# z's last four weight blocks and six of the output projection's in float32 products, without kept halves; the experts' early tiles five instead of three

## Chip, cores and metric

One Trainium2 chip, one core of it. The metric is the device time of one execution in microseconds (us); the kernel before has three runs, of which the median counts, and one profiled execution.

## What is computed

Two transformer blocks in float32 on 256 tokens of 1,024 features. The first block (stick-breaking attention, an RWKV-7 time mix and a gated feed-forward) is not touched. The second block, cut to what matters:

```python
u, z, xbc, dt = split(modulate(x) @ w_in)          # second input projection
y_pool = pool_mixer(u)                             # 256 columns
y_ssd  = rms(ssd(conv(xbc), dt) * silu(z)) * norm_w   # 768 columns, rms in 4 groups of 192
x = x + gate * (concat(y_pool, y_ssd) @ w_out)     # output projection
h = modulate(x)
x = x + gate * hier_moe(h, w13, w2)                # router, then 32 experts, top 2 in one group
```

## The kernel before

The work runs in stages on 128 tokens by up to 512 columns. Most large products are made in a reduced float format: a value is split into its rounding hi and the remainder lo (`wsplit`, L334, and `split_to`, L298: ScalarE rounds, L300, VectorE subtracts, L301), and `mm3` (L329) adds the three products hi*hi, hi*lo and lo*hi at L330 to L332. The experts' products (L1508 ph, L1571 pyo) take plain float32.

After the first block come four stages. *The second input projection* (`project`, L1130): for each chunk of 128 columns the weights, loaded two chunks to a tile (L350), are split and multiplied into `pi` (24 matmuls of 256 columns); `projected` (L1140) then makes the causal convolution, first ScalarE (L1146, `cva`), then three taps on VectorE (L1149), then the silu (L1150). The dt columns go through four small transposes (`pdt`, L1191) after the last chunk. *z*: `dense_rows` (L857) loads w_z in four tiles of two k each (L876), and multiplies block by block while the SSD (L1208 to L1241) runs between its products. Its argument `stag` says that the last four k keep their split halves, so that token block 0 can finish before block 1 uses the same halves. `fin_z` takes the silu of z, multiplies y, makes the four squares, a reciprocal root by some 13 small VectorE steps (L229 to L234), the scaling L1277, and turns y by transposes (`pyt`, L1281) into hi and lo (L1286, L1287). *The output projection*: the same `dense_rows` on w_out, with all eight k split, four of them kept in ring R; `fin_out` adds the result to x (L1374, L1375) and makes the router's product (`plg`, L1388). *The experts*: a tile of weights is 1 MB, six tiles an expert.

Expert tiles are loaded ahead of need by `fetch` (L1084), which SyncE issues in program order together with all other weights. `ORDER` names, one letter a tile, the buffers of the first 17: E is a ring of its own that exists early (`RING3` tiles), b pairs of half-size blocks, r the four-tile ring of all weight loads, R a ring of `RING2` tiles that exists from the output projection on; three more use a, w and x. `SOON` says how many tiles are fetched at three places (after the first chunks of the input projection, after the last, after the SSD), `EARLY` how many ahead of the output projection. A tile beyond these waits until its buffer is given back. The tile framework puts instructions of an engine in an order by its own planner, except where `issue_after` forces one.

Of the kernel before, what the change touches and what calls it, by code (L numbers as in the profile page):

```python
# [8 lines left out]
F32 = mybir.dt.float32  # L9
F32R = mybir.dt.float32r  # L10
# [21 lines left out]
BIG = 3.0e38  # L32
NEG = -3.0e38
RING = 4
RING2 = 5
RING3 = 3
ZROWS = 11
DT = 0
UP = 0
# [4 lines left out]
PO = 2  # L44
PD = 4
PZ = 2
PW = 1
WOSTAG = 4
SO = 6
SD = 5  # L50
WBUFS = 4
NB = 14
MIXG = 8
HALVES = 8
ORDER = "EEEbbbbRrrrrRRbRR"
EARLY = 8
ONCE = "awx"
SCHED = {}
RES = (29, 30)
R0 = (1,1,1,0,0,0)  # L60
SOON = (5, 5, 6)
AFT = (9, 12)
SCW = 4
WARM = (16, 4, 5, 2, 9)
PN = "mttp"
# [8 lines left out]
def two_blocks(ctx: ExitStack, tc: tile.TileContext, a: dict, out: bass.AP, dump=None, stop=""):  # L74
# [3 lines left out]
    def D_(name, ap):  # L78
        if dump is not None:
            dump(name, ap)  # L80
# [27 lines left out]
    def nm(s):  # L108
        uid[0] += 1
        return f"{s}{uid[0]}"  # L110
# [34 lines left out]
    def small(s, shape, dt=F32, tag=None, bufs=2):  # L145
        return (sc if shape[-1] <= SCW and len(shape) == 2 and shape[0] == P else ph["pool"]).tile(shape, dt, tag=tag or s, name=nm(s), bufs=bufs)
# [119 lines left out]
    def halves(t, n=512):  # L266
        return [t[:, 0:n], t[:, n : 2 * n]]
# [61 lines left out]
    def mm3(ps, lh, ll, rh, rl, first, last):  # L329
        pe.matmul(ps, lhsT=lh, rhs=rh, start=first, stop=False)  # L330
        pe.matmul(ps, lhsT=lh, rhs=rl, start=False, stop=False)  # L331
        pe.matmul(ps, lhsT=ll, rhs=rh, start=False, stop=last)  # L332

    def wsplit(src, n, alloc=None, eng=dve):  # L334
        hi, lo = (alloc or wblk)("wh"), (alloc or wblk)("wl")
# [136 lines left out]
    def hv(t, i):  # L472
        return t[:, i * 256 : (i + 1) * 256]
# [380 lines left out]
        D_(f"mTh{g}", mT[0][g]); D_(f"mTl{g}", mT[1][g])  # L854


    def dense_rows(w, nk, xT, finish, stag=2, keep=None, n=1024, pos=0, fill=None, after=()):  # L857
# [12 lines left out]

        pairs = list(range(0, nk, 2))
        first, last = pairs[: len(pairs) - stag // 2], pairs[len(pairs) - stag // 2 :]
        for n_, k0 in enumerate(first[:pos] + last + first[pos:]):
            t = raw("wrows")
            v = t[:, : 2 * n].rearrange("p (k c) -> p k c", k=2)
            sync.dma_start(out=t[:, : 2 * n], in_=w[k0 // 2])  # L876
            for j in range(2):
                with ExitStack() as st:
                    for at, ins in after:
                        if 2 * n_ + j >= at:  # L880
                            st.enter_context(tc.issue_after(ins))
                    hi, lo = wsplit(v[:, j, :], n, keep if k0 in last else wblk)
                if k0 in last:
                    kept.append((k0 + j, hi, lo))
                else:
                    go(0, k0 + j, hi, lo)
                    go(1, k0 + j, hi, lo)
        for k, hi, lo in kept:
            go(0, k, hi, lo)
        finish(0, acc[0])  # L890
        for k, hi, lo in kept:
            go(1, k, hi, lo)
        if fill:
            fill()
        finish(1, acc[1])
# [179 lines left out]
    def raw2(s_, dt=F32):  # L1075
        return ph["pool"].tile([P, 2048], dt, tag="raw2", name=nm(s_), bufs=RING2)
# [169 lines left out]
    fetch_n(SOON[2])  # L1246


    yT = act_T("mixT")
    for c in range(2):  # L1250
        ps = psm("ppool")
        for j in range(2):
            hs = slice(64 * j, 64 * j + 64)
            pe.matmul(ps[hs, 0:256], lhsT=wpool[hs, c, :], rhs=pw[hs, c, 16:272], start=True, stop=True)
        t = small("yp", [P, 256], bufs=2)
        dve.tensor_scalar(t, ps[:, 0:256], prm("pool_scale_2", c), None, op0=ALU.mult)
        split_to(atv(yT[0], c), atv(yT[1], c), t)
        D_(f"yp{c}", t)


    z_done = []

    def fin_z(tb, acc):
        sz = blk("sz")
        with tc.issue_after(last_exp.ins) if ZA else ExitStack():
            for hf in range(2):
                act.activation(sz[:, hf * 512 : hf * 512 + 512 - 256 * hf], acc[hf], AF.Silu)
        y = ysd[tb][:, 0:768]
        dve.tensor_tensor(y, y, sz[:, 0:768], ALU.mult)
        ss = small("gss", [P, 4])  # L1270
        for g in range(4):
            act.activation(sink[:, 0:192], y[:, g * 192 : g * 192 + 192], AF.Square, accum_out=ss[:, g : g + 1])
        v = small("gsv", [P, 4])
# [3 lines left out]
        z_done.append(dve.tensor_tensor(y3, y3, rk.rearrange("p (g o) -> p g o", o=1).to_broadcast([P, 4, 192]), ALU.mult).ins)  # L1277
        for g, n in ((0, 4), (1, 2)):
            pt = psm("pyt")
            for j in range(n):  # L1280
                pe.transpose(pt[:, j * P : (j + 1) * P], y[:, (4 * g + j) * P : (4 * g + j + 1) * P], ident)  # L1281
            for j in range(n):
                i = 4 * g + j
                src = pt[:, j * P : (j + 1) * P]
                hi, lo = (atv(yT[x], 2 + i, tb * P, tb * P + P) for x in range(2))
                act.activation(hi, src, AF.Copy, scale=prm("ssd_norm_w_2", i))  # L1286
                dve.scalar_tensor_tensor(lo, src, prm("ssd_norm_w_2", i), hi.bitcast(F32), op0=ALU.mult, op1=ALU.subtract)  # L1287
# [8 lines left out]
    kept = []  # L1296

    def keep(s_):
        if not kept:
            kept.extend(halves(raw2(s_, F32R), 1024))  # L1300
        return kept.pop(0)

    hn = [[blk("hnh", F32R), blk("hnl", F32R)] for _ in range(2)]
    lg = small("lg", [P, 2, 40], bufs=1)
# [456 lines left out]
```

## Time and profile before

| | us |
|---|---|
| runs | 1121.05, 1121.59, 1119.37 |
| median of the three | 1121.05 |
| the profiled execution | 1120.24 |
| its span on the core | 1118.5 |
| outside the span | 1.7 |

The mean granted TensorE clock of the profiled execution is 0.987. The span counts from the first to the last recorded instruction; times in rows are from its start. A TensorE row's length is that of one pipelined matmul, so of a series the steps between starts count, as the chain of waits gives them.

### The profile page before, as it was taken

The page shows a single profiled execution, that of the slowest core. Times are in us where ns is not written, and L with a number is a line of the kernel's source. Part 1 is how long each engine was busy: PE and PEld are TensorE (multiplying, and loading weights), DVE is VectorE, ACT ScalarE, POOL GpSimd, SP SyncE. Part 2 cuts the span into 40 slices and gives each one's busy share as a digit, 9 for nine tenths or more (in the row PEclk, how much of TensorE's full clock was granted, in tenths as well). Part 3 has the DMA queues.
Part 4 walks back from the last instruction along what each step waited for, and adds up shares of the span by engine and source line. Part 5 has one row for each costly group of instructions (what it writes and reads, how often), then busy time and mean ns, then how long its engine had stood idle before and what let it go on. Part 6 is the DMA issues. An engine that isn't in the chain of part 4 may idle for free.

```text
span 1118.5 us, 17553 instructions
## 1 busy us (share of the span) xinstructions
PE 1053.5 (94%) x7022; PEld 732.2 (65%) x7022; DVE 592.2 (53%) x1228; ACT 403.6 (36%) x713; POOL 82.0 (7%) x155
## 2 busy tenths in 40 slices
PE   8999999998799999999999889999999999999895
PEld 7988778896599999877997653444444444433332
DVE  5575975768778874555985653323232323222213
ACT  5454443454444444435665341121111111111113
POOL 4001600003200000004100000000000000000000
PEclk9999989999999999999999999999999999999998
DMA  9654520256566773636664599999999999999993
GB/s 328 219 214 163 193 81 16 101 181 234 196 256 227 263 287 121 253 113 227 247 208 151 184 326 419 410 419 416 416 421 416 415 420 417 416 419 417 417 418 150
DMA packets 57717, 313.01 MB, mean 280 GB/s; under 512 B 8864, under 2 KB 11040, under 8 KB 28064
## 3 DMA queue, kind: packets, MB, share of 16 engines
q1 hardware_dynamic: 53712, 286.50, 65.6%
q0 software_dynamic: 3456, 25.17, 6.1%
q8 instruction: 57, 0.93, 0.3%
q10 hardware_dynamic: 464, 0.17, 0.1%
q14 instruction: 28, 0.23, 0.1%
HBM read 310.77 MB, written 1.05 MB: 279 GB/s over the span
## 4 chain that ended last, share of the span: by engine, by line
PE 73%; DMA 15%; DVE 7%; ACT 2%; issue 2%; POOL 1%; SPq 0%; DVEq 0%; POOLq 0%; ACTq 0%
PE ph L1508 15%; DMA wexp<-in_w_dram 11%; PE pyo L1571 7%; PE acc L331 3%; PE acc L332 3%; PE acc L330 3%; PE moe L1589 2%; PE pga L1353 2%; DVE wl L301 2%; PE pfg L330 2%; PE pfg L331 2%; PE pfg L332 2%; PE pfu L331 2%; PE pfu L330 2%; PE pfu L332 2%
## 5 line engine op out<-in xcount | busy, mean ns | idle before, releaser
L1508 PE MATMUL ph<-wexp,xg 128*64 128x512 f32 x1024 | 229.5, 595 | 9.6 <-DMA wexp<-in_w_dram 9.0
L1508 PEld LDWEIGHTS ph<-wexp,xg 128*64 128x64 f32 x1024 | 71.8, 137 | 159.8 <-issue 129.3
L1571 PE MATMUL pyo<-wexp,gy 128*64 128x512 f32 x512 | 116.9, 599 | 2.6 <-DVE gy L1565 2.1
L1515 DVE TENSOR_TENSOR gy<-gy,ph 128x256 f32<-128x256 f32 x32 | 13.5, 421 | 152.2 <-ACT gy L1514 152.2
L1576 DVE SCALAR_TENSOR_TENSOR gy<-pyo,gs,g2h 128x512 f32<-128x512 f32 x32 | 24.0, 751 | 103.5 <-PE pyo L1571 103.5
L1571 PEld LDWEIGHTS pyo<-wexp,gy 128*64 128x64 f32 x512 | 34.1, 137 | 62.5 <-issue 53.7
L1514 ACT ACTIVATE gy<-ph 128x256 f32<-128x256 f32 x32 | 12.3, 383 | 165.0 <-PE ph L1508 165.0
L301 DVE TENSOR_TENSOR wl<-wrows,wh 128x1024 fp32r<-128x1024 f32 (+1 forms) x42 | 51.4, 1241 | 24.9 <-ACT wh L300 24.6
L301 DVE TENSOR_TENSOR wl<-wff,wh 128x1024 fp32r<-128x1024 f32 x44 | 55.1, 1253 | 17.2 <-ACT wh L300 17.1
L1580 ACT CAST yh<-gy 64x512 fp32r<-64x512 f32 x32 | 19.8, 618 | 115.6 <-DVE gy L1576 115.6
L300 ACT CAST wh<-wff 128x1024 fp32r<-128x1024 f32 x44 | 46.0, 1045 | 36.4 <-DMA wff<-in_w_ffn_dram 21.5
L300 ACT CAST wh<-wrows 128x1024 fp32r<-128x1024 f32 (+1 forms) x46 | 45.3, 1009 | 30.5 <-PE acc L331 21.7
L330 PE MATMUL pfg<-h2Th,wh 128*128 128x256 f32 x176 | 50.7, 288 | 0.1
L332 PE MATMUL pfg<-h2Th,wl 128*128 128x256 f32 x176 | 50.0, 284 | 0.0
L331 PE MATMUL pfu<-h2Tl,wh 128*128 128x256 f32 x176 | 49.9, 284 | 0.0
L330 PE MATMUL pfu<-h2Th,wh 128*128 128x256 f32 x176 | 49.9, 284 | 0.0
L332 PE MATMUL pfu<-h2Th,wl 128*128 128x256 f32 x176 | 49.9, 283 | 0.0
L331 PE MATMUL pfg<-h2Tl,wh 128*128 128x256 f32 x176 | 49.9, 283 | 0.0
L1353 PE MATMUL pga<-sel,hnh 128*128 128x256 f32 x128 | 33.1, 305 | 8.7 <-DVE sel L1347 7.0
L332 PE MATMUL pi<-h3Th,wl 128*128 128x256 f32 (+1 forms) x136 | 38.7, 284 | 1.8 <-DVE wl L301 1.8
L331 PE MATMUL pi<-h3Tl,wh 128*128 128x256 f32 (+1 forms) x136 | 38.6, 284 | 0.0
L330 PE MATMUL pi<-h3Th,wh 128*128 128x256 f32 (+1 forms) x136 | 38.6, 284 | 0.0
(555 smaller groups left out, 2593.1 us busy)
## 6 DMA issues: line engine op xcount, KB each, us to landing
wexp<-in_w_dram SPq DMA_DIRECT2D x134, 1024.0 KB, 15.2
wexp<-in_w_dram SPq DMA_DIRECT2D x116, 512.0 KB, 12.7
wada<-in_w_ada_dram POOLq DMA_DIRECT2D x24, 1024.0 KB, 5.3
wff<-in_w_ffn_dram SPq DMA_DIRECT2D x22, 1024.0 KB, 5.9
wrows<-in_w_ffn_down_dram SPq DMA_DIRECT2D x11, 1024.0 KB, 5.4
wg<-in_w_in_dram SPq DMA_DIRECT2D x8, 1024.0 KB, 4.9
wi<-in_w_in_dram SPq DMA_DIRECT2D x8, 1024.0 KB, 5.6
wrw<-in_w_in_dram SPq DMA_DIRECT2D x6, 1024.0 KB, 9.3
```

The source lines that it names most:

```text
L300: act.copy(hi, src)
L301: eng.tensor_tensor(lo, src, hi.bitcast(F32), ALU.subtract)
L330: pe.matmul(ps, lhsT=lh, rhs=rh, start=first, stop=False)
L331: pe.matmul(ps, lhsT=lh, rhs=rl, start=False, stop=False)
L332: pe.matmul(ps, lhsT=ll, rhs=rh, start=False, stop=last)
L1353: return pe.matmul(ps, lhsT=hn[tb][part][:, k * P : (k + 1) * P], rhs=sel[tb].rearrange("p (e j s) -> p e j s", e=GE, j=2)[:, :, 0, :], st ...
L1508: last = pe.matmul(ph_[64 * t_ : 64 * t_ + 64, :], lhsT=xg[k // 4][:, (k % 4) * 256 + el * CAP : (k % 4) * 256 + el * CAP + CAP], rhs=wa[k ...
L1515: dve.tensor_tensor(g, g, ph_[:, 256:512], ALU.mult)
L1571: last = pe.matmul(py_[64 * t_ : 64 * t_ + 64, :], lhsT=gT[:, (kc % 2) * P + (kc // 2) * 64 : (kc % 2) * P + (kc // 2) * 64 + 64], rhs=wb[ ...
L1576: dve.scalar_tensor_tensor(y32, py_, gs, g2h, op0=ALU.mult, op1=ALU.mult)
L1580: act.copy(y[hi], y32[hi])
L1589: last = pe.matmul(acc[tb][hf], lhsT=sT[:, tb * P : (tb + 1) * P], rhs=ys[hf], start=(e == 0), stop=(e == E - 1))
```

## The change

The last four k of z are no longer split: the raw float32 weight rows are multiplied with `h3f`, the sum of the activations' hi and lo, in one float32 product each (L868 of the changed kernel). The output projection has code of its own, `out_rows`: y is kept in float32 (`yf`) for k 0, 1 and 4 to 7, which are multiplied with the raw rows (L1481), and in hi and lo (`y23`) for k 2 and 3, whose weights are still split. k 0 and 1 (the pool's part) come first for both token blocks; then y of block 0 is scaled and turned, k 2 and 3 of block 0, y of block 1 is scaled and turned, the rest of block 0, and block 1. The rings hold five E and three R tiles instead of three and five; `SOON` fetches seven tiles at the first place instead of five.

```diff
-RING2 = 5
-RING3 = 3
+RING2 = 3
+RING3 = 5
-PW = 1
-WOSTAG = 4
-ORDER = "EEEbbbbRrrrrRRbRR"
-EARLY = 8
+ORDER = "EEEEEbbbbRRRrrbrr"
+EARLY = 9
-SOON = (5, 5, 6)
-AFT = (9, 12)
+SOON = (7, 7, 8)
...
+                if lo is None:
+                    pe.matmul(acc[tb][hf], lhsT=hv(whole, k % 4)[:, t0:t1], rhs=hi[:, sl], start=ndone[tb] == 0, stop=ndone[tb] == nk - 1)
+                    continue
...
+                if whole is not None and k0 in last:
+                    kept.append((k0 + j, v[:, j, :], None))
+                    continue
...
-    dense_rows(a["w_z"], KC, h3T, fin_z, 4, lambda s_: ph["pool"].tile([P, 768], F32R, tag="keep", name=nm(s_), bufs=8), 768, PZ)
+    h3f = pconst("h3f", [P, 1024])
+    dve.tensor_tensor(h3f, h3T[0][1].bitcast(F32), h3T[1][1].bitcast(F32), ALU.add)
+    dense_rows(a["w_z"], KC, h3T, fin_z, 4, None, 768, PZ, whole=h3f)
...
-    dense_rows(a["w_out_2"], KC, yT, fin_out, WOSTAG, keep, pos=PW, after=list(zip(AFT, z_done)))
+    def out_rows():
...
+        w23 = [wsplit(w[k], 1024) for k in (2, 3)]
+        fetch_n(EARLY + RING2)
...
+                if k in (2, 3):
...
+                    last = mm3(acc[tb][hf], yh, yl, halves(hi)[hf], halves(lo)[hf], False, False)
+                else:
+                    last = pe.matmul(acc[tb][hf], lhsT=hv(yf[k // 4], k % 4)[:, t0:t1], rhs=halves(w[k])[hf], start=k == 0, stop=k == KC - 1)
...
+        for k in range(2):
+            for tb in range(2):
+                go(tb, k)
+        scaled(0)
+        turn = turned(0)
+        for k in (2, 3):
+            last = go(0, k)
+        with tc.issue_after(turn.ins):
+            scaled(1)
+        with tc.issue_after(last.ins):
+            turned(1)
+        for k in range(4, KC):
+            go(0, k)
+        fin_out(0, acc[0])
+        for k in range(2, KC):
+            go(1, k)
+        fin_out(1, acc[1])
```

How it moves instructions, in three places. The first is SyncE's queue in the second input projection, before (wi are the projection's tiles, wexp the experts'; a half tile has 1024 columns):

```order
L1092 DMA wexp_5838<-in_w_2_dram 128x2048
L1092 DMA wexp_5840<-in_w_2_dram 128x2048
L1092 DMA wexp_5842<-in_w_2_dram 128x2048
L350 DMA wi_6010<-in_w_in_dram 128x2048
L350 DMA wi_6082<-in_w_in_dram 128x2048
L1098 DMA wexp_5844<-in_w_2_dram 128x1024
L1098 DMA wexp_5845<-in_w_2_dram 128x1024
L1098 DMA wexp_5848<-in_w_2_dram 128x1024
L1098 DMA wexp_5849<-in_w_2_dram 128x1024
L350 DMA wi_6154<-in_w_in_dram 128x2048
L350 DMA wi_6226<-in_w_in_dram 128x2048
```

and in the changed kernel:

```order
L1097 DMA wexp_5838<-in_w_2_dram 128x2048
L1097 DMA wexp_5840<-in_w_2_dram 128x2048
L1097 DMA wexp_5842<-in_w_2_dram 128x2048
L1097 DMA wexp_5844<-in_w_2_dram 128x2048
L1097 DMA wexp_5846<-in_w_2_dram 128x2048
L1103 DMA wexp_5848<-in_w_2_dram 128x1024
L1103 DMA wexp_5849<-in_w_2_dram 128x1024
L1103 DMA wexp_5852<-in_w_2_dram 128x1024
L1103 DMA wexp_5853<-in_w_2_dram 128x1024
L347 DMA wi_6014<-in_w_in_dram 128x2048
L347 DMA wi_6086<-in_w_in_dram 128x2048
```

The two late input tiles (wi_6010 and wi_6082 before, wi_6014 and wi_6086 now) had three expert tiles ahead of them and now have five and two pairs of halves.

The second is ScalarE in the same stage, around the first split of the late input tile, before (CAST wh is a split, the ACTIVATE from pi the convolution's start, into BT or CT the silu):

```order
L1150 ACTIVATE BT_5649<-cva_5897 128x256
L300 CAST wh_6013<-wi_6010 128x1024
L1146 ACTIVATE cva_5969<-pi_5940,par 128x256
L1150 ACTIVATE BT_5649<-cva_5932 128x256
L300 CAST wh_6048<-wi_6010 128x1024
L1146 ACTIVATE cva_6004<-pi_5975,par 128x256
L1150 ACTIVATE CT_5650<-cva_5969 128x256
```

and in the changed kernel:

```order
L1155 ACTIVATE BT_5649<-cva_5901 128x256
L1151 ACTIVATE cva_5973<-pi_5944,par 128x256
L1155 ACTIVATE BT_5649<-cva_5936 128x256
L1155 ACTIVATE CT_5650<-cva_5973 128x256
L1151 ACTIVATE cva_6008<-pi_5979,par 128x256
L297 CAST wh_6017<-wi_6014 128x1024
L1155 ACTIVATE CT_5650<-cva_6008 128x256
```

The split of the late tile (wh_6013 before, wh_6017 now) stood ahead of the convolution of the chunk two before its own (pi_5940); now it stands behind that of the chunk right before its own (pi_5979). On VectorE the remainder wl of this split stands behind that convolution's three taps in the same way.

The third is TensorE in the output projection, where y's transposes come, before (acc are the sums of the two token blocks by two halves):

```order
L330 MATMUL acc_6771<-wh_6790,mixTh_6490 128x512
L331 MATMUL acc_6771<-wl_6791,mixTh_6490 128x512
L332 MATMUL acc_6771<-wh_6790,mixTl_6492 128x512
L1281 MATMUL pyt_6650<-ident,ysd_6308 128x128 x4
L1281 MATMUL pyt_6663<-ident,ysd_6308 128x128 x2
L330 MATMUL acc_6768<-wh_6824,mixTh_6490 128x512
L331 MATMUL acc_6768<-wl_6825,mixTh_6490 128x512
```

and in the changed kernel:

```order
L1481 MATMUL acc_6645<-wrows_6647,mixT_6494 128x512
L1481 MATMUL acc_6646<-wrows_6647,mixT_6494 128x512
L1293 MATMUL pyt_6694<-ident,ysd_6312 128x128 x4
L1293 MATMUL pyt_6705<-ident,ysd_6312 128x128 x2
L327 MATMUL acc_6643<-wh_6655,mixT_6496 128x512
L328 MATMUL acc_6643<-wl_6656,mixT_6496 128x512
L329 MATMUL acc_6643<-wh_6655,mixT_6496 128x512
```

Before, the products ahead of the transposes are hi/lo ones of k 0 and 1; now they are float32 ones (L1481), eight in all, and the hi/lo products of k 2 follow.

## Rows read from the trace of the kernel before

**Rows 1.** The page: busy time, traffic by slice (40), the last chain by engine.

```profile
PE 1053.5 (94%) x7022; PEld 732.2 (65%) x7022; DVE 592.2 (53%) x1228; ACT 403.6 (36%) x713; POOL 82.0 (7%) x155
...
GB/s 328 219 214 163 193 81 16 101 181 234 196 256 227 263 287 121 253 113 227 247 208 151 184 326 419 410 419 416 416 421 416 415 420 417 416 419 417 417 418 150
...
PE 73%; DMA 15%; DVE 7%; ACT 2%; issue 2%; POOL 1%; SPq 0%; DVEq 0%; POOLq 0%; ACTq 0%
```

**Rows 2.** The chain of waits, 940 to 1000 us: start, us, what.

```profile
943.11 6.87 PE ph L1508 x32
...
952.62 17.41 DMA wexp<-in_w_dram
...
970.10 13.19 DMA wexp<-in_w_dram
```

**Rows 3.** By window: length; PE, PEld, DVE, ACT, POOL busy; granted clock, DMA share, GB/s.

```profile
680.00:720.00 40.00, 39.48 (x203) 17.51 (x199) 12.36 (x22) 7.84 (x15) 0.00 (x0) 1.00 1.01 415
```

**Rows 4.** Timeline of SyncE's queue, 606 to 665 us: first start, time over all, issues.

```profile
646.85 9.46 SPq L1098 DMA_DIRECT2D wexp<-in_w_dram  x6
659.37 2.04 SPq L1092 DMA_DIRECT2D wexp<-in_w_dram  x2
```

**Rows 5.** The chain of waits, first expert matmuls.

```profile
657.39 7.09 PE ph L1508 x32
```

**Rows 6.** By window: second input projection, z, output projection.

```profile
538.00:569.42 31.42, 31.42 (x262) 31.36 (x262) 28.90 (x47) 21.75 (x37) 0.00 (x0) 1.00 0.55 191
569.49:608.58 39.09, 39.09 (x234) 31.91 (x233) 25.06 (x48) 21.39 (x45) 0.00 (x0) 1.00 0.54 187
608.58:642.12 33.54, 29.25 (x134) 22.47 (x132) 21.75 (x61) 15.86 (x42) 0.19 (x1) 0.95 0.49 177
```

**Rows 7.** Timeline of ScalarE, 543.5 to 550.8 us.

```profile
543.56 1.05 ACT L300 CAST wh<-wi 128x1024 fp32r<-128x1024 f32 x1 [0.95 <-PE pi L331]
...
546.44 1.05 ACT L300 CAST wh<-wi 128x1024 fp32r<-128x1024 f32 x1 [1.06 <-PE pi L331]
547.40 0.56 ACT L1146 ACTIVATE cva<-pi,par 128x256 f32<-128x256 f32 x1
```

**Rows 8.** Timeline of VectorE, 543.5 to 551.7 us (x3: three taps together).

```profile
544.64 1.23 DVE L301 TENSOR_TENSOR wl<-wi,wh 128x1024 fp32r<-128x1024 f32 x1
545.78 1.51 DVE L1149 SCALAR_TENSOR_TENSOR cva<-pi,par,cva 128x255 f32<-128x255 f32 x3
```

**Rows 9.** Timeline of SyncE's queue, 518 to 545 us.

```profile
518.89 1.46 SPq L1092 DMA_DIRECT2D wexp<-in_w_dram  x3
523.83 6.17 SPq L350 DMA_DIRECT2D wi<-in_w_in_dram  x2
```

**Rows 10.** By window, the first expert's loads.

```profile
658.00:668.00 10.00, 8.90 (x46) 3.19 (x44) 1.99 (x11) 2.88 (x6) 0.00 (x0) 1.00 0.82 291
```

**Rows 11.** The chain of waits in the output projection.

```profile
622.53 0.43 PE acc L331
...
625.85 0.23 PE acc L330
...
627.02 0.66 PE pyt L1281 x6
...
634.66 0.54 PE ptr L1380 x4
...
636.56 0.82 PE plg L1388 x8
```

**Rows 12.** TensorE's waits, 600 to 645 us: in all, times, longest.

```profile
PE pyt L1281 <- DVE gsv L1274: 2.2, 1, 2.2
PE acc L331 <- DVE wl L301: 1.5, 1, 1.5
```

**Rows 13.** By window, around an idle stretch of TensorE.

```profile
256.90:260.20 3.30, 0.02 (x2) 0.01 (x1) 3.30 (x4) 0.78 (x1) 3.30 (x3) 1.00 0.87 330
261.00:264.00 3.00, 3.00 (x12) 2.20 (x11) 3.00 (x4) 1.97 (x3) 3.00 (x3) 0.54 0.95 371
```

More of the change, by code (lines that the diff above doesn't have):

```diff
@@ L331, in mm3 @@
         pe.matmul(ps, lhsT=lh, rhs=rl, start=False, stop=False)
-        pe.matmul(ps, lhsT=ll, rhs=rh, start=False, stop=last)
+        return pe.matmul(ps, lhsT=ll, rhs=rh, start=False, stop=last)
     def wsplit(src, n, alloc=None, eng=dve):
@@ L854, in two_blocks, with dense_rows @@
         D_(f"mTh{g}", mT[0][g]); D_(f"mTl{g}", mT[1][g])
-    def dense_rows(w, nk, xT, finish, stag=2, keep=None, n=1024, pos=0, fill=None, after=()):
+    def dense_rows(w, nk, xT, finish, stag=2, keep=None, n=1024, pos=0, fill=None, after=(), whole=None):
         acc = [[f("acc") for _ in range(2)] for f in (pm, pt_)]
@@ L1246, in two_blocks @@
     fetch_n(SOON[2])
-    yT = act_T("mixT")
+    yf, y23 = [ablk("mixT", F32) for _ in range(2)], ablk("mixT")
     for c in range(2):
@@ L1254, in two_blocks @@
             pe.matmul(ps[hs, 0:256], lhsT=wpool[hs, c, :], rhs=pw[hs, c, 16:272], start=True, stop=True)
[L1255 to L1261, printed above, removed]
+        dve.tensor_scalar(hv(yf[0], c), ps[:, 0:256], prm("pool_scale_2", c), None, op0=ALU.mult)
+    z_sums = []
     def fin_z(tb, acc):
@@ L1272, in fin_z, with scaled @@
             act.activation(sink[:, 0:192], y[:, g * 192 : g * 192 + 192], AF.Square, accum_out=ss[:, g : g + 1])
+        z_sums.append(ss)
+    def scaled(tb):
+        y, ss = ysd[tb][:, 0:768], z_sums[tb]
         v = small("gsv", [P, 4])
@@ L1276, in fin_z, with turned @@
         y3 = y.rearrange("p (g c) -> p g c", g=4)
-        z_done.append(dve.tensor_tensor(y3, y3, rk.rearrange("p (g o) -> p g o", o=1).to_broadcast([P, 4, 192]), ALU.mult).ins)
+        dve.tensor_tensor(y3, y3, rk.rearrange("p (g o) -> p g o", o=1).to_broadcast([P, 4, 192]), ALU.mult)
+    def turned(tb):
+        y = ysd[tb][:, 0:768]
         for g, n in ((0, 4), (1, 2)):
@@ L1284, in fin_z @@
                 src = pt[:, j * P : (j + 1) * P]
-                hi, lo = (atv(yT[x], 2 + i, tb * P, tb * P + P) for x in range(2))
-                act.activation(hi, src, AF.Copy, scale=prm("ssd_norm_w_2", i))
-                dve.scalar_tensor_tensor(lo, src, prm("ssd_norm_w_2", i), hi.bitcast(F32), op0=ALU.mult, op1=ALU.subtract)
-    dense_rows(a["w_z"], KC, h3T, fin_z, 4, lambda s_: ph["pool"].tile([P, 768], F32R, tag="keep", name=nm(s_), bufs=8), 768, PZ)
+                if i < 2:
+                    hi, lo = (hv(y23, 2 * x + i)[:, tb * P : tb * P + P] for x in range(2))
+                    act.activation(hi, src, AF.Copy, scale=prm("ssd_norm_w_2", i))
+                    dve.scalar_tensor_tensor(lo, src, prm("ssd_norm_w_2", i), hi.bitcast(F32), op0=ALU.mult, op1=ALU.subtract)
+                else:
+                    o = hv(yf[(2 + i) // 4], (2 + i) % 4)[:, tb * P : tb * P + P]
+                    if i % 2:
+                        last = dve.tensor_scalar(o, src, prm("ssd_norm_w_2", i), None, op0=ALU.mult)
+                    else:
+                        act.activation(o, src, AF.Copy, scale=prm("ssd_norm_w_2", i))
+        return last
+    h3f = pconst("h3f", [P, 1024])
+    dve.tensor_tensor(h3f, h3T[0][1].bitcast(F32), h3T[1][1].bitcast(F32), ALU.add)
+    dense_rows(a["w_z"], KC, h3T, fin_z, 4, None, 768, PZ, whole=h3f)
     close_phase()
     open_phase("final")
[L1296 to L1301, printed above, removed]
     hn = [[blk("hnh", F32R), blk("hnl", F32R)] for _ in range(2)]
@@ L1445, in two_blocks, with go @@
     fetch_n(EARLY)
-    dense_rows(a["w_out_2"], KC, yT, fin_out, WOSTAG, keep, pos=PW, after=list(zip(AFT, z_done)))
+    def out_rows():
+        acc = [[f("acc") for _ in range(2)] for f in (pm, pt_)]
+        w = []
+        for k0 in range(0, KC, 2):
+            t = raw("wrows")
+            sync.dma_start(out=t, in_=a["w_out_2"][k0 // 2])
+            w += halves(t, 1024)
+        w23 = [wsplit(w[k], 1024) for k in (2, 3)]
+        fetch_n(EARLY + RING2)
+        def go(tb, k):
+            t0, t1 = tb * P, tb * P + P
+            for hf in range(2):
+                if k in (2, 3):
+                    hi, lo = w23[k - 2]
+                    yh, yl = (hv(y23, 2 * x + k - 2)[:, t0:t1] for x in range(2))
+                    last = mm3(acc[tb][hf], yh, yl, halves(hi)[hf], halves(lo)[hf], False, False)
+                else:
+                    last = pe.matmul(acc[tb][hf], lhsT=hv(yf[k // 4], k % 4)[:, t0:t1], rhs=halves(w[k])[hf], start=k == 0, stop=k == KC - 1)
+            return last
+        for k in range(2):
[15 more added lines that the diff above has]
+        fin_out(1, acc[1])
+    out_rows()
     def gate_weights():
```

## Prediction

> **What bounds the kernel now.** I read the page first. TensorE is busy for 94% of the span, yet the chain that ended last is 15% DMA, and the traffic stands at some 415 GB/s in every slice after the 24th [rows 1]. The chain near its end says why. Until 952.6 us it runs over the experts' matmuls; from there it is a sequence of expert tiles, each piece ending just as the next begins [rows 2]. The share of the DMA engines from 680 to 720 us is already 1.01 at 415 GB/s [rows 3]. So the end is set by a stream of expert tiles that nothing in this change makes shorter: a tile of 1.05 MB takes 2.5 us at that rate, and six of them (15 us) take longer than the 13 us of an expert's matmuls.
>
> When does that stream begin? Twenty tiles fit in the buffers (17 by the order string, three more in a, w and x). SyncE issues the last that wait for the router at 646.85 us and after, and the first tile that needs a buffer that an expert gave back at 659.37 us [rows 4], two us after the first expert matmul, which stands in the chain at 657.39 us [rows 5]. From there each tile waits for a release, and releases follow the first expert matmul. **So the end moves with the start of the experts, one for one**, and tiles that land earlier than now buy nothing by themselves. The prediction is therefore a sum over the three stages ahead of 657.39 us: the second input projection, z, and the output projection [rows 6]. In the first two TensorE has no idle time at all (31.42 of 31.42 and 39.09 of 39.09 us), in the third it is busy for 29.25 of 33.54 us.
>
> **The projection: a new wait, +2.8 us.** Before, ScalarE rounds the weights of the chunk that comes next (wh, 1.05 us) before it starts the convolution of the chunk that just ended: at 546.44 us the split, at 547.40 the convolution of the chunk that ended at 546.4, as one chunk earlier at 543.56 us [rows 7]. VectorE does the same, its remainder wl at 544.64 us ahead of three taps at 545.78 [rows 8]. TensorE never waits. In the changed order one pair has traded places: the first wh of the late input tile stands behind the convolution of the chunk before it, and its wl behind that convolution's three taps. That convolution needs the chunk's last matmul, at about 546.4 us. From there: 0.1 to start, 0.56 for the convolution, 1.51 for the taps, 1.23 for wl, 0.1 for hand-overs: TensorE's third product of the next chunk, due at about 546.7 us, starts at about 549.9. That is 3.1 us. The four small transposes of dt (0.3 us) now fall into the hole and leave the place after the projection, so 2.8 us net. After it the chain is again one chunk ahead (the next split needs only the hole's time, and one chunk has 24 matmuls of 0.12 us, 2.9 us), so I count the hole once. Bounds: 0, were the order of no effect, and 3.1.
>
> The tiles themselves are not late. Now three expert tiles go out at 518.89 us and the input tile at 523.83 [rows 9]; in the change five tiles and two pairs of halves (7 MB instead of 3) are ahead of it. At 2.5 us per tile that is 10 us more: the late input tile lands at some 542 us, against a first use at 547. The margin is 4 to 5 us; even at the 291 GB/s of a slower stretch [rows 10] the 8.4 MB would be there at 547.7 us, under 1 us late. The following tiles have more.
>
> **z: +1.9 us.** The last four k of z are 8 groups (four k, two token blocks) of 768 columns. As three products of the hi/lo halves, 512 columns take 0.23 us a product, as the output projection's rows at full clock show [rows 11], and 256 half of that: 3 x 0.35 = 1.05 us a group. A float32 product of 512 columns is costed from the experts: 32 records in 6.87 us [rows 2], and these are 8 whole 128-column products (each two halves of 64 columns side by side, two records a half), so 0.86 us each; 1.29 us a group with the 256. The difference is 0.24 us, times 8 is 1.9 us. I take all of it, since TensorE has no slack in this stage. The four pairs of splits that leave ScalarE and VectorE there cost nothing now (TensorE covered them), so they give nothing back. The sum of hi and lo into h3f is one VectorE instruction of some 1.2 us (as wl of the same 1024 columns, [rows 8]) hidden by matmuls long before its use. Bounds: +1 us, if a few of the switches between kinds of matmul go, and +3, if the SSD's steps, now closer together, wait for ScalarE's exponentials once.
>
> [...] The expert row gives 0.86 us, less than four times the 0.23 us of one product, and I go by the row.
>
> **The output projection: -2.6 us.** TensorE's work now: 24 float32 products (six k, two token blocks, two halves) at 0.86 = 20.6 us; 8 groups of three for k 2 and 3 at 0.70 = 5.6; two sets of six transposes at 0.66; between them the first token block's two sets of transposes at some 0.5 and two halves of the router product at 0.82 [rows 11]. Together 30.1 us. Before, this stretch took 33.54 us, of which 4.3 idle [rows 6]: 2.2 for y's scaling before its transposes, 1.5 for the split of a weight block [rows 12]. Nine or ten products near 622 us ran at half the clock, 0.43 us instead of 0.23 [rows 11], another 2 us. Both go. The splits on VectorE that made them are no longer there. The wait for y's scaling shrinks too: token block 0 of z now ends 4 x 1.29 = 5.2 us ahead of the stage, its squares fall under block 1's products, and 6.9 us of k 0 and 1 follow, where now 24 products of 0.23, 5.5 us, and then the 2.2 us of waiting stand. So no wait of over 0.5 us is left there, one of some 0.3 to 0.5 for each set of transposes to be copied out, as now. 33.5 - 30.1 = 3.4, less 0.8 for these waits: -2.6 us. Bounds: -3.4, and -1 if block 1's scaling, now queued on VectorE behind block 0's copies, is late by 1.5 us.
>
> **Rings.** Five early and three late tiles instead of three and five hold the same 17; the expert loop sees the same 20 tiles ahead. The last two tiles ahead of the router still wait for the projection's last matmuls. I give this nothing.
>
> **Sum:** +2.8 + 1.9 - 2.6 = +2.1 us. The profiled execution took 1120.24 us, 0.8 below the median of the three runs, 1121.05; the sum gives 1122.3 against the one and 1123.2 against the other. I say **1122.7 us**. About 0.2% (2.2 us) is what a measurement of this kernel can tell from no change, so this is a small loss at the edge of what shows.
>
> **Rivals.**
> 1. *Slower: the clock falls in the new hole.* After 3.3 us without matmuls at 257 us the granted clock stood at 0.54 from 261 to 264 us [rows 13]; after the waits of 614 to 622 us products took 0.43 us. [...] For it: the hole is as long as the one at 614 us. Against: before and after it TensorE is wholly busy, which it was not in either case. [...] 20%.
> 2. *Faster: the stream fills sooner.* From 658 to 668 us the engines moved 291 GB/s instead of 415 [rows 10], 1.2 MB less: 3 us. In the change the late tiles of the first ring are loaded at z's end and not at 636 to 642 us, so the queue is short when the experts begin, and the first refills may land with less delay. Were all of this won, 1119.7; with the output projection at its full -3.4, 1118.9. Against: it is the releases, not the queue, that those refills wait for. 20%.
> 3. *Slower: a whole float32 product is dearer than two half-width ones side by side.* Priced as four of the 0.23 us products [rows 11], it takes 0.93 us instead of 0.86: 24 x 0.07 = 1.7 us in the output projection and 8 x 1.5 x 0.07 = 0.8 in z, together 2.5: 1125.2. It decides from 0.9 us a product. For it: no row of before has such a product of 128 columns by 512. Against: the array's width has cost nothing in any other row. [...] 10%.
> 4. *No effect in the projection.* If the split is not held up by the order, the hole is 0 and the sum -0.7: about 1120. 5%.
>
> **Chances.** The forecast has 45%, the four rivals 55%. The range takes the forecast's bounds (the output projection at -1 and z at +3 give +4.8, at -3.4 and +1 with the hole +0.4) and rivals 1 and 3, and leaves the corners: 1118.2 to 1126.0 us. Faster by over 0.2% needs the whole of rival 2 or 4 and the output projection near its full gain: 12 of rival 2's 20% and 3 of rival 4's 5, so 15%. Slower by over 0.2% is rivals 1 and 3 and about a sixth of the forecast's weight: 38%. Within it: 47%.
>
> **What would show it.** Right: a TensorE wait of about 3 us behind wl near 547 us, no idle of over 1 us in the output projection, no row at 0.43 us for its hi/lo products, float32 products 0.86 us apart, z's stage near 41 us and the output projection near 31, the first expert matmul at about 659.5 us, and the chain's end in expert tiles as now. Wrong: no wait at 547 us, a new one in z behind an exponential, the engines at 415 GB/s from 658 us on, or an end that does not follow that matmul.

## The result, and the profile after

The changed kernel takes 1128.42 us (median of 8 runs, 1125.55 to 1130.06); the kernel before, beside it on the same chip, 1119.80 us (8 runs, 1118.95 to 1122.65). The ratio is 1.007 [1.0055, 1.0084]: **slower by 8.6 us**. The forecast was a loss of 2 us (1122.7 us, range 1118.2 to 1126.0): the direction was right, the size and the range were not.

The profiled execution of the changed kernel took 1128.82 us against 1120.24 before; its span is 1127.1 us and its mean granted clock 0.980 (0.987 before). Page of the changed kernel, the lines of [rows 1]:

```profile
PE 1064.3 (94%) x6982; PEld 732.0 (65%) x6982; DVE 582.2 (52%) x1213; ACT 394.2 (35%) x697; POOL 83.2 (7%) x155
...
GB/s 325 209 213 164 201 76 40 95 167 224 203 254 227 257 269 164 218 126 245 280 175 87 242 247 415 414 417 416 418 417 418 419 416 418 418 417 416 419 417 145
...
PE 67%; DMA 21%; DVE 8%; issue 2%; ACT 2%; POOL 0%; DVEq 0%; SPq 0%; POOLq 0%; ACTq 0%
```

TensorE has 40 records less and is busy 10.8 us longer: the same work at a lower clock, or dearer work. The stream of tiles from the 25th slice on is what it was. Where the time went stands in the windows of the changed kernel, to be laid beside [rows 6]: the second input projection, z, the output projection, and from there to the first expert matmul (length; PE, PEld, DVE, ACT, POOL busy; granted clock, DMA share, GB/s):

```profile
539.16:575.46 36.30, 33.74 (x267) 33.31 (x268) 29.02 (x49) 20.57 (x35) 0.00 (x0) 0.95 0.58 221
575.46:616.50 41.04, 40.75 (x213) 29.91 (x212) 22.55 (x47) 20.96 (x48) 0.00 (x0) 1.00 0.32 112
616.50:647.78 31.28, 31.04 (x111) 17.48 (x109) 13.37 (x45) 7.95 (x24) 0.19 (x1) 1.00 0.63 250
647.78:665.43 17.65, 13.41 (x87) 12.65 (x87) 13.76 (x56) 8.43 (x19) 2.69 (x3) 0.81 0.72 253
```

The fourth stretch, whose code is not touched, stood in no row of the prediction. Before, it was this:

```profile
642.12:657.39 15.27, 10.68 (x86) 9.97 (x86) 13.53 (x56) 8.47 (x19) 2.64 (x3) 1.00 0.93 339
```

With one set of marks for all kernels the two profiled executions differ as in the table, in us. The marks are starts: of the first and the last `pi` matmul (input projection), of the third silu `sz` on ScalarE (end of z), of the third `go` on VectorE (end of the output projection) and of the first expert matmul `ph` (end of the router). The ends lie within 0.9 us of those of the windows above, which show the input projection only from 538 or 539 us on.

| | before | after | difference |
|---|---|---|---|
| start of the input projection | 518.13 | 519.29 | +1.2 |
| input projection | 51.15 | 56.04 | +4.9 |
| z | 39.14 | 41.32 | +2.2 |
| output projection | 33.00 | 30.31 | -2.7 |
| router | 15.97 | 18.47 | +2.5 |
| first expert matmul at | 657.39 | 665.43 | +8.0 |
| from there to the last `ph` | 441.02 | 441.11 | +0.1 |

The first line is chance: the block before is the same code, and the start of the input projection varies from 516.3 to 521.9 us over the profiles of this study. The last line shows that the end follows the first expert matmul one for one. The line of the output projection rests on one profile of the kernel before: a second one, shown further down, took 31.49 us there instead of 33.00. The end of the chain of waits of the changed kernel is, as in [rows 2], a sequence of expert tiles (start, us, what):

```profile
1059.04 17.39 DMA wexp<-in_w_dram
...
1076.49 12.58 DMA wexp<-in_w_dram
...
1089.11 1.94 PE ph L1564 x8
```

**The hole.** The timelines of ScalarE and of VectorE in the changed kernel show the order that the prediction walked through, against [rows 7] and [rows 8]. ScalarE:

```profile
547.77 0.56 ACT L1151 ACTIVATE cva<-pi,par 128x256 f32<-128x256 f32 x1
548.23 1.03 ACT L297 CAST wh<-wi 128x1024 fp32r<-128x1024 f32 x1
```

VectorE:

```profile
548.39 1.51 DVE L1154 SCALAR_TENSOR_TENSOR cva<-pi,par,cva 128x255 f32<-128x255 f32 x3
549.81 1.21 DVE L298 TENSOR_TENSOR wl<-wi,wh 128x1024 fp32r<-128x1024 f32 x1
```

TensorE's waits from 540 to 560 us in the changed kernel (us in all, times, longest) are the two halves of the hole:

```profile
PE pi L327 <- ACT wh L297: 1.3, 1, 1.3
PE pi L329 <- DVE wl L298: 1.3, 1, 1.3
```

And what follows the hole was only a rival of the prediction: the granted clock falls. The window behind it, and the matmuls there in the chain of waits, which step by 0.21 us where 0.12 is their step at full clock:

```profile
552.00:555.50 3.50, 3.50 (x19) 3.50 (x18) 0.59 (x1) 0.26 (x1) 0.00 (x0) 0.51 0.60 202
```

```profile
540.00 0.12 PE pi L329
...
554.14 0.21 PE pi L327
...
555.94 0.12 PE pi L328
```

A stretch like this row's 3.50 us, in which TensorE is busy throughout at a granted clock of 0.51, costs about half of its length, some 1.7 us (an estimate: 0.49 of 3.50 us; by the steps of 0.21 and 0.12 us it is 1.5). Below, "a fall" is one such stretch.

**The output projection** does what was forecast. Its products in the changed kernel's chain, beside [rows 11]:

```profile
617.05 6.87 PE acc L1481 x16
623.91 0.45 PE pyt L1293 x4
...
626.00 0.23 PE acc L328
...
629.53 0.66 PE pyt L1293 x6
630.19 5.15 PE acc L1481 x12
```

Six float32 products are 12 records in 5.15 us, 0.86 each; the hi/lo products stand at 0.23, none at 0.43, and TensorE is busy for 31.04 of 31.28 us. But behind the stage the clock falls, after a wait that was there before too (the gather `pga` for the index `gi`). That wait before, then the waits from 612 to 666 us and two windows of the changed kernel:

```profile
PE pga L1353 <- DVE gi L1326: 1.7, 1, 1.7
```

```profile
PE pga L1368 <- DVE gi L1341: 1.9, 1, 1.9
PE ptr L1395 <- DVE x L1390: 1.3, 2, 0.7
```

```profile
658.00:664.00 6.00, 5.30 (x26) 5.14 (x26) 3.15 (x14) 0.00 (x0) 0.00 (x0) 0.50 0.62 231
667.00:677.00 10.00, 8.90 (x44) 3.17 (x42) 1.11 (x5) 1.94 (x3) 0.00 (x0) 1.00 0.81 278
```

From 658 to 664 us the granted clock is 0.50. The second window shows what became of the hope that the stream fills sooner: the engines move 278 GB/s there, [rows 10] had 291.

### The profile page after: what moved, and what is told of

Read it like the earlier page. It is cut to its first block, busy times and chain, and to the rows that moved or that the text cites. A ratio compares the mean times of both kernels' runs of the same rounds, so it can differ in the third digit from the quotient of the medians.

```text
span 1127.1 us, 17434 instructions
## 1 busy us (share of the span) xinstructions
PE 1064.3 (94%) x6982; PEld 732.0 (65%) x6982; DVE 582.2 (52%) x1213; ACT 394.2 (35%) x697; POOL 83.2 (7%) x155
## 4 chain that ended last, share of the span: by engine, by line
PE 67%; DMA 21%; DVE 8%; issue 2%; ACT 2%; POOL 0%; DVEq 0%; SPq 0%; POOLq 0%; ACTq 0%
DMA wexp<-in_w_dram 18%; PE ph L1564 11%; PE pyo L1627 6%; PE acc L328 2%; PE acc L327 2%; PE acc L329 2%; DVE wl L298 2%; PE moe L1645 2%; PE pfg L327 2%; PE pga L1368 2%; DMA wada<-in_w_ada_dram 2%; PE pfu L328 2%; PE pfu L327 2%; PE pfu L329 2%; PE pfg L329 2%
## 5 line engine op out<-in xcount | busy, mean ns | idle before, releaser
L298 DVE TENSOR_TENSOR wl<-wrows,wh 128x1024 fp32r<-128x1024 f32 (+1 forms) x36 | 45.2, 1273 | 25.1 <-ACT wh L297 25.1
L297 ACT CAST wh<-wrows 128x1024 fp32r<-128x1024 f32 (+1 forms) x36 | 36.0, 1026 | 32.7 <-PE acc L328 22.1
```

## Experiments

All medians stand beside runs of the kernel before on the same chip. Falls are counted in windows of 2 us of the profiled executions. Each stage's time is measured by the marks of the table above.

**One part alone: the hole.** The kernel before, with only the first split of the late tile forced behind the convolution and its taps:

```diff
-        hi, lo = wsplit(v[:, :, ci * P : ci * P + m], m, alloc, eng)
+        if late:
...
+            with tc.issue_after(behind[0]):
+                act.copy(hi, src)
+            with tc.issue_after(behind[1]):
+                dve.tensor_tensor(lo, src, hi.bitcast(F32), ALU.subtract)
...
-                dense_T(v, KC, h3T, j, m, ps[:m, :256], pool if c0 in PP and j else dve)
+                dense_T(v, KC, h3T, j, m, ps[:m, :256], pool if c0 in PP and j else dve, late=c0 == 2560 and j == 0)
```

> The kernel before with one thing of the change: the split of the first block of the late input tile is put behind the convolution of the chunk before (ScalarE) and behind its taps (VectorE), as the changed kernel has it. Theory: the hole of TensorE near 547 us is 2.5 to 3.1 us, the granted clock falls to about 0.5 for some 4 us behind it (2 us more), and the end follows: 3 to 5 us above before. Rival (the hole is made up for in the later stages, or only the float32 products matter): within 1 us of before. If the clock stays at 1.00 behind the hole, the fall in the changed kernel came from something else.

Measured: 1123.78 us against 1119.80, ratio 1.0044 [1.0028, 1.0059], +4.0 us. The input projection took 55.82 us instead of 51.15. TensorE waits there for 2.0 us in three parts (1.3, 0.4 and 0.3; forecast 2.5 to 3.1), so this hole is a little shorter than that of the changed kernel. By window:

```profile
546.00:548.00 2.00, 0.51 (x2) 0.30 (x2) 1.89 (x6) 2.00 (x4) 0.00 (x0) 1.00 0.19 74
548.00:550.00 2.00, 1.60 (x8) 1.40 (x9) 1.98 (x2) 0.35 (x2) 0.00 (x0) 0.82 0.00 0
550.00:552.00 2.00, 2.00 (x12) 2.00 (x11) 0.00 (x0) 0.00 (x0) 0.00 (x0) 0.50 0.58 134
552.00:554.00 2.00, 2.00 (x16) 2.00 (x16) 0.00 (x0) 0.78 (x1) 0.00 (x0) 0.83 0.65 246
```

The order alone makes a hole, and the hole brings a fall. It holds nearly half of the whole loss.

**All but the hole.** The changed kernel, with five tiles fetched at the first place instead of seven, so that the late input tile has fewer ahead of it:

```diff
-SOON = (7, 7, 8)
+SOON = (5, 7, 8)
```

> The changed kernel with five expert tiles fetched at the first place instead of seven; the order of ScalarE and VectorE in the input projection is then that of before. Theory: no wait of TensorE near 547 us, no fall of the clock there, so 4.5 to 5 us below the changed kernel, 3 to 4 above before; what is left is z (+1.9), the output projection (-2.4), and the router stage at half clock (+2.4), if the clock falls there again. Rival (the rings or the float32 products cost the 8.6 us): at most 1 us below the changed kernel.

Measured: 1123.18 us (12 runs), ratio 1.0021 [1.0008, 1.0034], +3.4 us, so 5.2 us less than the change. The input projection is back at 51.14 us. The output projection has its 30.34 us, the router a fall at 652 to 658 us. But z took 44.36 us, and its windows show two falls where TensorE has no idle time (the second of them at 598 to 602 us):

```profile
590.00:592.00 2.00, 2.00 (x7) 1.18 (x8) 0.56 (x1) 1.36 (x4) 0.00 (x0) 0.88 0.00 0
592.00:594.00 2.00, 2.00 (x5) 1.30 (x5) 1.12 (x2) 1.72 (x4) 0.00 (x0) 0.50 0.00 0
594.00:596.00 2.00, 2.00 (x14) 1.48 (x13) 0.00 (x0) 0.00 (x0) 0.00 (x0) 0.77 0.00 0
```

**z alone.** The kernel before, with z's last four k as float32 products and no kept halves:

```diff
+                if lo is None:
+                    pe.matmul(acc[tb][hf], lhsT=hv(whole, k % 4)[:, t0:t1], rhs=hi[:, sl], start=ndone[tb] == 0, stop=ndone[tb] == nk - 1)
+                    continue
...
+    dense_rows(a["w_z"], KC, h3T, fin_z, 4, None, 768, PZ, whole=h3f)
```

> The kernel before with z's last four k in float32 products against h3f, all else as before. Theory: the z stage grows by 1.9 us (39.1 to 41.0), the router stage stays at 15.3 us with the clock at 1.00, so 1.5 to 2.5 us above before. Rival (float32 products are what lets the clock fall later): the router stage shows a clock of 0.5 and takes over 17 us. Rival (the splits that go give something back): no slower than before.

Measured: a median of 1130.88 us, ratio 1.0092 [1.0062, 1.0121], but of six executions two stand at 1122 and four at 1130 to 1134. The profile was of one at 1121.95 us: z took 42.01 us without a fall, +2.9 against the forecast +1.9, and the first expert matmul came at 658.80. So the work costs 1 us more than was forecast, and something else comes and goes.

**The output projection alone.** The kernel before, with `out_rows` of the change; z, rings, `ORDER` and `SOON` as before.

> The output projection of the changed kernel alone, with z and all rings and fetches as before. Theory: the output projection takes 31 us instead of 33.5 and the end follows, 2 to 3 us below before, if the clock stays up in the router stage. Rival (the float32 products ahead of the router lower its clock): the stage from the last product to the first expert matmul takes 17.6 us instead of 15.3, at a clock of 0.5, and the time is within 1 us of before.

Measured: 1120.33 us, ratio 0.9998 [0.9985, 1.0011]. The stage is 3 us shorter (30.05 us against 33.00), and nothing of it is left at the end. The windows of the router say where it went:

```profile
648.00:650.00 2.00, 0.89 (x5) 0.92 (x6) 1.90 (x8) 1.11 (x2) 0.41 (x1) 0.83 0.99 334
650.00:652.00 2.00, 2.00 (x11) 2.00 (x11) 1.27 (x12) 0.30 (x2) 0.00 (x0) 0.50 0.96 283
652.00:654.00 2.00, 1.82 (x14) 1.69 (x12) 0.39 (x4) 0.00 (x0) 0.00 (x0) 0.82 1.01 391
```

The router took 17.49 us instead of 15.97, and in this execution the input projection began 1.3 us later (519.41 against 518.13), so that the first expert matmul stood at 657.42 against 657.39 us. That start is chance, and the runs show no gain either. Against the 31.49 us of the second profile of the kernel before, the stage is only 1.4 us shorter, which the router's +1.5 takes back.

**z alone, twice more, and the two kernels again.** Single profiled executions, for how often the clock falls:

> The kernel of e3 once more, for a look at one of its slow executions (four of six took 1130 to 1134 us, with a lower clock over the whole span). Theory: the extra 8 to 10 us are stretches at half clock in the z stage, which the change makes possible: the SSD's short products stand close together there, so the z stage takes 45 to 50 us. Rival: the clock is lost in the first block or in the output projection, and the z stage stays at 42 us.

> The kernel of e3 a third time, for a look at an execution of 1130 us or more. Theory: more falls of the clock in the z stage than the one of e5, so that it takes 45 us or more. Rival: the z stage takes 42 to 44 us and the rest lies in stages that the change does not touch.

> The changed kernel once more, for a second look. Theory: the hole near 547 us with half clock behind it is there again, since the order is fixed; the falls in the z stage and in the router stage may come and go. Rival: the hole or its half clock is missing, so that part of the 8.6 us was chance.

> The kernel before, a second look. Theory: no wait and no fall of the clock in the input projection and the z stage (51.15 and 39.1 us), one fall in the output projection (33 us). Rival (falls in z are chance in any kernel): the z stage shows one here too and takes 40.8 us or more.

Measured: z alone 1125.01 and 1127.13 us, with one fall in z each (43.57 and 43.59 us, against 42.01 without). The changed kernel again: 1130.70 us, two falls behind the hole (57.25 us), two in z (44.49), none in the router (16.23). The kernel before again: 1119.19 us, its stages within 0.1 us of the first profile but for the output projection (31.49 instead of 33.00 us). No profile of z alone caught an execution above 1130 us, and in neither of these two did z take the 45 us or more that their theories wanted. In the three profiles of z alone the output projection, whose code is that of before, took 33.4 to 33.8 us, in two of them with two falls: this kernel loses time there too. And both profiles of the kernel before have one fall in the output projection, in one of 33.00 us and in one of 31.49: in the first TensorE is busy for 4.00 of 4.00 us of it (622 to 626 us, clock 0.54 and 0.60), in the second for 4.43 of 6.00 (616 to 622 us, 0.80, 0.50 and 0.84). That a fall costs less where TensorE waits while it lasts is argued from these two.

What does TensorE do ahead of a fall in z? Its timeline in the second profile of the changed kernel, every line from 591.73 until 595.07 us being of the same two kinds (products of 64 columns for `pys`, products from 44 rows and `cneg` for `pcs`):

```profile
591.73 0.33 PE L1243 MATMUL pys<-xdt,ee 128*128 128x64 f32 x2
...
593.11 0.43 PE L1235 MATMUL pcs<-cs,pick 44*128 44x384 f32 x1
...
594.84 0.39 PE L1236 MATMUL pcs<-cneg,identr 128*128 128x256 f32 x1
595.07 0.43 PE L329 MATMUL acc<-wh,h3Tl 128*128 128x512 f32 x1
...
595.94 0.63 PE L327 MATMUL acc<-wh,h3Th 128*128 128x512 f32 x1
```

The products for `acc` behind them run at a granted clock of 0.50 (596 to 598 us), those of 256 columns 0.21 us apart instead of 0.12, and these are still hi/lo products: no float32 product of z has run yet (the first comes at 604.33 us). The same holds for the second fall there and for those of z alone, four of the seven falls in z. In the two kernels with all but the hole the float32 products begin at 583 us, ahead of their three falls. So a float32 product of z isn't needed for a fall. Nor does the order settle it: the first profile of the changed kernel has the same rows from 590.01 to 593.12 us, and the products for `acc` behind them at a clock of 1.00, 0.12 us apart. The same SSD rows stand in the kernel before, mixed with more of z's products; its timeline has these:

```profile
592.75 0.39 PE L1241 MATMUL pys<-xdt,ee 128*128 128x64 f32 x2
592.94 0.36 PE L330 MATMUL acc<-wh,h3Th 128*128 128x256 f32 x1
...
595.29 0.39 PE L1241 MATMUL pys<-xdt,ee 128*128 128x64 f32 x2
595.61 0.44 PE L1230 MATMUL pcs<-cs,pick 44*128 44x384 f32 x1
```

There, eleven products for `acc` stand from 592.94 to 594.67 us. Between the first `pcs` and the last `pys` of z lie 61 or 62 records of z's products in the kernels with split halves, 34 or 44 in those with float32 ones.

**Dummies in the router.** The kernel has small matmuls of no use (`warm`, into `pga` and others) that keep TensorE busy (32 records of them take 3.82 us below). Fourteen more of them ahead of the gather, once with the output projection alone and once with all but the hole:

```diff
-WARM = (16, 4, 5, 2, 9)
+WARM = (16, 4, 19, 2, 9)
```

> The kernel of e4 with 14 more dummy products of 128 columns ahead of the first gather of rows in the router stage, where TensorE waits 1.7 us for VectorE. Theory (that wait lets the clock fall, which takes back what the output projection gains): clock 1.00 through the router stage, that stage 15.3 to 16 us instead of 17.5, and 1.5 us below e4, 2 to 3 below before. Rival (the fall comes from the float32 products, or the dummies delay the gather): no gain over e4.

> The kernel of e2 with the same 14 dummy products in the router stage. Theory: 1.5 us below e2, at about 1121.5, with falls of the clock left in the z stage alone. Rival: as e2.

Measured: 1119.14 us (ratio 0.9990 [0.9976, 1.0004]) and 1122.16 us (1.0019 [0.9999, 1.0038]). The router has no fall in either, but takes 17.24 us: too many dummies. They now end after the index is there, and the gather waits for them, as the timeline of the first shows:

```profile
644.60 3.82 PE L366 MATMUL pga<-ident 128*128 128x128 f32 x32
648.18 1.20 PE L1366 MATMUL pga<-sel,hnh 128*128 128x256 f32 x8
```

So six more instead of fourteen, with the output projection alone:

```diff
-WARM = (16, 4, 5, 2, 9)
+WARM = (16, 4, 11, 2, 9)
```

> The kernel of e6 with 6 dummy products more than before instead of 14. In e6 the clock stayed up, but the dummies ended 1.2 us after the gather could have begun. Theory: 6 fit into the 1.7 us wait, the clock stays at 1.00, the router stage takes 16.0 us as before, and the time is 1 us below e6, about 1.5 to 2 us below before. Rival (the wait that is left lets the clock fall): the stage takes 17.5 us again, as in e4.

Measured: **1118.14 us** (12 runs) against 1120.10, ratio 0.9978 [0.9968, 0.9989]: 2 us (0.2%) faster than the kernel before, and the fastest kernel of the study. The kernel before with the same six dummies was not run; neither of its two profiles has a fall in the router. The router takes 15.99 us at the full clock, and the wait that was 1.7 us is 0.4. Window of the router and TensorE's wait:

```profile
650.00:656.00 6.00, 5.00 (x42) 4.69 (x40) 4.94 (x23) 0.46 (x3) 0.00 (x0) 1.00 0.82 277
```

```profile
PE pga L1366 <- DVE gi L1339: 0.4, 1, 0.4
```

**Dummies in z.** z alone, with five dummies ahead of each group of `pcs` products but the first:

```diff
+            if g and r_ == 0:
+                warm(5, ps)
```

> The kernel of e3 with five dummy products of 128 columns (1.1 us) put among the short products of each of the last three groups of the SSD. Theory (the clock falls in z because the SSD's short products stand too close, though TensorE never waits): no fall between the projection's end and the output projection; the z stage takes 42.0 + 3.4 = some 45.4 us in every look. Rival (the float32 products of z let it fall): falls of 1.7 us as in e5 and e11 on top, 47 us or more. Three looks, of which this is the first.

> The second look at the kernel of e12. Theory (short products too close): no fall of the clock in the z stage, which takes some 45.4 us. Rival (the float32 products let it fall): a fall there, 47 us or more.

> The third look at the kernel of e12. Theory (short products too close): no fall of the clock in the z stage, which takes some 45.4 us. Rival (the float32 products let it fall): a fall there, 47 us or more.

Measured: 1127.45 us (4 runs, 1126.23 to 1129.74; ratio 1.0051 [1.0034, 1.0067]); the second and third profiled executions took 1131.7 and 1127.9 us. In all three profiles z has no fall and takes 44.6 us: in z the dummies cost 2.6 us over the 42.0 of z alone without a fall, more than the one fall of 1.6 (43.6 less 42.0) that they spare. Whether they pay over many runs isn't shown: the kernel stands 6.2 us above before, z alone stood 11.1 above, on another chip. The second and third profiles each had a fall in the router (17.50 and 17.36 us), and all three have two falls in the output projection (34.0 to 34.4 us). The planner's order changes with the dummies (the first float32 product of z now comes behind the last `pys`), so they aren't the only difference.

The count of falls over all profiles:

| place | kernels | profiles with a fall |
|---|---|---|
| behind the hole | with the hole | 3 of 3 |
| | without | 0 of 13 |
| z | hi/lo products | 0 of 6 |
| | float32 products | 5 of 7 (7 falls) |
| | float32 products and dummies | 0 of 3 |
| output projection | hi/lo products | 9 of 9 |
| | float32 products | 0 of 7 |
| router | 5 dummies there, as before | 5 of 13 |
| | 11 or 19 | 0 of 3 |

Over runs, the parts alone add to 4.0 + 11.1 + 0.5 us, more than the 8.6 of the whole: z alone holds most of the excess, by its executions above 1130 us. Split the other way the sum holds by construction: all but the hole is +3.4 us, and the hole on top +5.2.

## Why the prediction was wrong

- **What bounds the kernel: right.** From the first expert matmul to the last `ph` lie 440.0 to 441.2 us in every profile of the study, whatever stood ahead. Of the 8.6 us between the two profiled executions 8.0 had arisen by the first expert matmul.
- **The hole: right as a wait, too small as a price.** The order held back the split and the remainder as described, and where TensorE had no wait it now has two of 1.3 us. The stage grew by 4.9 us; with 1.7 of that for the fall, 3.2 remain, against 2.8 net and 3.1 gross (from the prediction's own times, 546.7 and 549.9 us, the gross is 3.2). Rival 1, the clock falling in the new hole, had 20%. The price that the range counts for it no run shows; measured, one fall cost 1.6 to 1.7 us (43.57 less 42.01 in z, the estimate of 0.49 of 3.50 behind the hole). The rival came true in all three profiles with the hole. The argument against it, that TensorE is wholly busy before and after, did not hold: it is, and the clock fell all the same after a wait of 2.6 us in two parts, and after one of 2.0 us in three where the order was moved alone. The order alone cost 4.0 us in runs.
- **The input tiles: right that they don't make the wait, wrong in the margin.** The first late tile, issued at 531.66 us, landed 14.1 us later, at 545.8 and not at some 542. The split began at 548.23, straight behind the convolution, so the tile was there 2.4 us ahead instead of 4 to 5. In the former order the split would have stood near 544.7 (an estimate: 543.56 of [rows 7] and the 1.2 us of the later start), some 1 us ahead of the tile. What that would have cost TensorE no run shows; in the kernel before the tile landed at 532.4 us, 8.6 after its issue; the kernel with the hole alone keeps those fetches, and there the order made the hole.
- **z: right as work, wrong as a stage.** The float32 products take 0.86 us each, so rival 3 (0.93 us) is out. Its price of four hi/lo products was the author's estimate; the trace shows 0.86 against 0.23 us, 3.7 times. The stage grew by 2.2 us in the change and by 2.9 in z alone where no fall came, against 1.9 and bounds of 1 to 3. What was missed is the clock: in five of seven profiles with float32 products in z it falls once or twice, 1.6 us each (44.49 us with two in the changed kernel, 41.32 with none), in a stage in which TensorE waits for 0.3 us at most. The prediction looked for a rise in waits there and took a busy TensorE for one at full clock.
- **The output projection: right as work, by luck on the number, and worth nothing.** -2.7 us against -2.6 (-2.3 by the windows of [rows 6]), 0.24 us of idle time, no product at half the clock, 31.28 us. But the 33 us that it is measured from hold a fall that landed on TensorE's work; against the 31.49 us of the second profile of before it is -1.2. And the router's stage behind it, which was counted as unchanged, gave it back: +2.5 us in the changed kernel's profile, +1.5 in the output projection alone, whose runs show no gain (0.9998 [0.9985, 1.0011]). The waits there are the old ones; now the clock falls at one of them, in three of the four profiles with this output projection and the old dummies. With six more dummies the gain is there: 1118.14 us, 2.0 below before.
- **Rings: nothing that shows.** No run changes them alone; from the first expert matmul on the two kernels take the same time. Rival 2 (the stream fills sooner) did not show: 278 GB/s in the first expert's window. The fetches that came with the rings are what moved the split, which the prediction counted under the projection.

**The step that failed** is thus one: every term was priced at the clock of the row that it came from, the full one but for the half-clock products that the change removed, and the clock was allowed to answer the change in one place, at 20%. In the changed kernel's profile, falls are some 1.7 us behind the hole and 2.5 in the router, 4.2 of 8.0 us (its z had none; the second profile of it had two there, two behind the hole and none in the router). The rest sums to +3.2 + 2.2 - 2.7 = +2.7 us, close to the forecast +2.1, and the 1.2 us upstream of all of it are chance. How close is luck in part: the -2.7 holds the fall that the profile of before had there, and from the other profile the sum would be +4.2.

Three things stay open. z alone had executions of 1130 to 1134 us at a mean clock of 0.975 to 0.978 that no profile caught; that they are more falls is argued from the clock alone, and the falls need not lie in z: the one profile above 1130 us of a kernel like it, the second with dummies in z (1131.7 us), has none there, but two in the output projection, one in the router and a start at 521.9 us. That the falls in z come from SSD products standing closer together is argued from what precedes them and from the dummies' effect; a kernel that spaces them by order alone was not tried. And that the router's fall follows from the output projection's is argued from a few profiles: two of the nine with hi/lo products in the output projection have one there too.

## What to carry to other kernels

Price a new wait of TensorE with what its clock does after it: here 2.0 to 2.6 us of waiting cost 4 to 5. When a stage loses its idle time or its clock fall, read the next stage's waits before counting the gain, because an old wait may now bring the fall there (here one of 1.7 to 1.9 us, with a clock of 0.50 behind it in three of four profiles); a few cheap dummies in that wait can keep it away, but only as many as end before the data arrives (here six left the router at 15.99 us, fourteen made it 17.24). A dense stretch is no proof of a full clock (in z it stood at 0.50 with TensorE busy for 2.00 of 2.00 us): look at the granted clock in windows of 2 us, over more than one execution.

## What was unexpected

- The granted clock fell to 0.50 in z while TensorE was busy for 2.00 of 2.00 us in each of the three windows ahead (588 to 594 us in the changed kernel's second profile), with no more than one wait of 0.3 us in z (1.71 of 2.00 us busy from 586 to 588 us) and none in the kernel with all but the hole. Ahead of five of the seven falls the timelines show short products back to back, as the `pys` and `pcs` from 591.73 to 595.07 us above. Rows overlap (the `pcs` at 593.11 us is 0.43 us long, and the next row starts at 593.47), so a stretch that is busy throughout in its rows is no proof that TensorE had no gap.
- Falls in unchanged code come and go between executions of one kernel: the input projection began between 516.3 and 521.9 us behind the same first block, and the router, with its dummies as before, had a fall in 5 of 13 profiles.
- The falls went with the work: all nine profiles with hi/lo rows in the output projection have one or two falls there, all seven with float32 rows none, and three of the four of those without more dummies have one in the router. Two of the nine have one in both places.
